# Hybrid trunk on one core: first squares folded on VectorE, first modulation group by k tile, rstd read from PSUM

## The chip, the cores and the metric

The kernel runs on one core of one Trainium2 chip. The metric is the device time of one execution in microseconds (us); lower is better. A core has five engines with a queue each, which run in parallel and wait for each other by semaphores: TensorE (PE, matmuls from SBUF into PSUM), VectorE (DVE), ScalarE (ACT), GpSimd (POOL) and SyncE (SP, which here issues the DMA transfers). Each queue is worked off in its own order.

## What is computed

Two layers of a decoder trunk over 256 tokens of width 2048, in float32:

```python
c_act = silu(c)
for l in range(2):
    shift, scale, gate = split(c_act @ w_ada[l] + b_ada[l], 3)
    h = rms_norm(x, norm_w[l]) * (1 + scale) + shift
    gq, gk, gv, ..., aq, ak, av, az = split(h @ w_in[l])
    o = concat(gated_linear_attention, gated_delta_net, differential_attention)   # each normed and gated
    x = x + gate * (o @ w_out[l])
```

`w_ada` is 2048 x 6144 per layer (the modulation), `w_in` 2048 x 7704 (the input projection), `w_out` 2048 x 2048.

## The kernel before

Tokens lie on the free axis of `xt` (128 features x 16 k tiles x 256 tokens). All weights are streamed from HBM in pieces of 128 x 1024 (512 KB) through six buffers of one pool (`raw` for projections, `rawa` for modulation, both with the tag "raw").

**Projections** are made in split precision: `weights` loads a piece, ScalarE casts it to `wh` (fp32r), VectorE makes the rest `wl = raw - wh`; three buffers each. `project` then issues per k tile three matmuls, `wh`x`hh`, `wl`x`hh` and `wh`x`hl`, where `hh` and `hl` are the two halves of the modulated h, made by `modulate`: VectorE multiplies x, the rstd row and the scale (`hn`), ScalarE adds the shift (`hh`), VectorE takes the rest (`hl`). `BLOCKS` lists 28 blocks of output columns (18 to 27 are token blocks `aq`, `ak`, `av`, `gz`, `dz`, `az` of 512 columns) and `STEPS` the groups of blocks and k tiles in which they are done: in layer 0 first blocks 18 to 27 on k tiles 0 and 1 ("group 0"), then the same on k tiles 2 and 3 ("group 1"), then the rest. `in_chunks` cuts a group into pieces of 1024: in group 0 one block with both k tiles per piece, ten pieces, 12 matmuls each. The accumulators `pt` and `pf` share four PSUM banks (tag "p"); the first group of a block is copied out by ScalarE, later ones are added by VectorE (`evac_`).

**Modulation** runs on VectorE: each piece of `w_ada` is multiplied by the row of c (`c_row`) and summed along its columns (`ada_group`, the line with `accum_out`); eight pieces make a group, and four small ScalarE instructions finish it (`ada_j`). Groups 0 to 7 of a layer give scale and shift of two k tiles each, groups 8 to 11 the gates. The pieces of a layer's first group 0 (`fr`) are loaded at the very start; all others are spread over the program by `advance` and `pace`.

**rstd** (`rstd_rows`): the squares of x are made by ScalarE in four quarters and folded by GpSimd, TensorE sums them over partitions into `ss`, ScalarE and GpSimd (`row_power`) make r, ScalarE spreads r on the diagonal of `dg`, TensorE multiplies ones by it into `rstd_ps`, and ScalarE copies that to `rb` in SBUF, which `modulate` reads. In layer 1 the squares come from the end of layer 0's output projection.

The GLA, GDN and attention parts run as generators between the projections' pieces (`poll`). The tile framework's scheduler sets each engine's order from the code's order, priorities (`AHEAD`, `URG`) and its own simulated times; only matmuls that share an accumulator group are pinned by hand (`in_order`). Small constants (`load_constants`: the rest of `ct`, `adb`, `posi`) are loaded when the first block is done.

Of the kernel before, what the change touches and what calls it, by code (L numbers as in the profile page):

```python
# [75 lines left out]
def in_chunks(layer, i):  # L76

    b0, b1, k0, k1 = STEPS[layer][i]
    out = []
    for b in range(b0, b1):  # L80
# [60 lines left out]
def hybrid_trunk(ctx: ExitStack, tc: tile.TileContext, x, cvec, pos, par, w_ada, w_in, w_out, w_lr, qkn, adt, cst, out):  # L141
# [91 lines left out]
    in_order = lambda: tc.manual_schedule(engines={mybir.EngineType.PE})  # L233
# [3 lines left out]
    SP.dma_start(pt, par)  # L237
# [8 lines left out]
    SP.dma_start(ct[:, 0:128], cst[:, 0:128])  # L246
# [3 lines left out]
    first_raws = []  # L250
# [39 lines left out]
    state = {"n": 0}  # L290

    def weights(src, n):

        raw = wraw.tile([P, RAW], F32, name="raw", tag="raw")[:, 0:n]
        wh = wsp.tile([P, RAW], F32R, name="wh", tag="wh")[:, 0:n]
        wl = wsp.tile([P, RAW], F32R, name="wl", tag="wl")[:, 0:n]
        with tc.high_priority(offset=AHEAD if state["n"] else 0):
            SP.dma_start(raw, src)
# [3 lines left out]
        state["n"] += 1  # L302
        return wh, wl

# [8 lines left out]
    def ada_group(l, g, raws=None):  # L313

        sums = tiny("ada_p", 8)
        for i in range(8):
            if raws is None:
                raw = wraw.tile([P, RAW], F32, name="rawa", tag="raw")[:, 0:1024]
                with tc.high_priority(offset=AHEAD):
                    SP.dma_start(raw, w_ada[l, g, i])  # L320
            else:
                raw = raws[i]
            cb = c_row[:, 1024 * (i % 2):1024 * (i % 2) + 1024]
            with tc.high_priority(offset=AHEAD):
                DVE.scalar_tensor_tensor(raw, raw, 1.0, cb, ALU.mult, ALU.mult, accum_out=sums[:, i:i + 1])  # L325
            if i < 7:
                yield
        for f in range(4):
            if g < 8:
                k = 2 * g + f % 2  # L330
                j = 0 if f < 2 else 1
            else:
                k = 4 * (g - 8) + f
                j = 2
            o, scale = ada[l][:, j, k:k + 1], pcol("norm", 16 * l + k) if j == 0 else 1.0
            bias = pcol("b_ada", 48 * l + (16, 0, 32)[j] + k)
            ACT.activation(tiny("ada_j", 2), sums[:, 2 * f:2 * f + 2], AF.Identity, bias=bias, scale=scale, accum_out=o)  # L337
        yield

    def ada_all():  # L340
        for l in range(L):
            for g in range(12):
                yield from ada_group(l, g, first_raws if l == 0 and g == 0 else None)

    ada_it = ada_all()
    ada_n = [0]
# [14 lines left out]
    def rstd_rows(sqs):  # L361
# [21 lines left out]
    def modulate(l, xt, rb, hh, hl, k):  # L383

        for i in range(k, k + 2):
            h = reg(i % 4, "hn")[:, 0:T]
            scale, shift = ada[l][:, 0, i:i + 1], ada[l][:, 1, i:i + 1]
            DVE.scalar_tensor_tensor(h, rb, scale, xt[:, i, :], ALU.mult, ALU.mult)
            ACT.activation(hh[:, i, :], h, AF.Identity, bias=shift)  # L389
            DVE.scalar_tensor_tensor(hl[:, i, :], h, shift, hh[:, i, :].bitcast(F32), ALU.add, ALU.subtract)  # L390


    in_off = [0]
# [894 lines left out]
```

## Time and profile before

| | |
|---|---|
| median of 3 runs (lowest, highest) | 1103.11 us (1100.97, 1106.03) |
| the profiled execution's own time | 1103.98 us |
| its span in the profile | 1102.2 us |
| busy PE, DVE, ACT, POOL | 1047.0, 888.6, 607.2, 219.8 us |
| moved by DMA | 273.24 MB, mean 248 GB/s |

A busy share is an average over stages with different limits; a matmul's end is modelled, so TensorE counts as busy while matmuls overlap. "Idle before" in brackets says how long the engine stood still before an instruction and what ended that. In a group of matmuls the spacing of their starts, not their length, is the rate.

### The profile page before, as it was taken

What the parts mean: (1) busy time and instruction counts of PE and PEld (TensorE: products, weight loads), DVE (VectorE), ACT (ScalarE), POOL (GpSimd) and SP (SyncE); (2) the same over time, 40 slices, a digit from 0 to 9 for tenths busy, and PEclk for the clock granted to TensorE, in tenths of its full rate; (3) what the DMA queues carried; (4) which work ended last, traced back from release to release, by engine and by line L of the source; (5) the groups of instructions that cost most, each with busy time, mean ns of one, the idle gap of its engine ahead of it and who ended that gap; (6) DMA issues with size and microseconds to landing.
All of it is one profiled execution on the core that took longest, in us unless ns stands there. A gap on an engine that the chain in (4) does not pass through costs nothing.

```text
span 1102.2 us, 19699 instructions
## 1 busy us (share of the span) xinstructions
PE 1047.0 (95%) x7398; PEld 918.9 (83%) x7398; DVE 888.6 (81%) x1365; ACT 607.2 (55%) x1251; POOL 219.8 (20%) x284
## 2 busy tenths in 40 slices
PE   4999999999899989999979999999999999999998
PEld 3768888889898777898977877899989877889998
DVE  5899999998999886888687776677756776787874
ACT  4745544447765646466545555468444556557742
POOL 4000000040130841134210000024222144102400
PEclk9999999999999999999998999999999999999999
DMA  9888999999877545755588888796535645777472
GB/s 352 311 299 308 351 336 341 329 296 339 301 270 254 182 145 188 249 162 186 167 318 327 308 315 319 238 306 228 181 116 174 218 164 172 246 244 236 136 216 90
DMA packets 76799, 273.24 MB, mean 248 GB/s; under 512 B 8816, under 2 KB 9888, under 8 KB 76576
## 3 DMA queue, kind: packets, MB, share of 16 engines
q1 hardware_dynamic: 76704, 271.99, 71.7%
q8 instruction: 58, 0.95, 0.3%
q14 instruction: 37, 0.30, 0.1%
HBM read 267.76 MB, written 4.19 MB: 247 GB/s over the span
## 4 chain that ended last, share of the span: by engine, by line
PE 55%; DVE 18%; DMA 11%; issue 9%; ACT 5%; POOL 2%; SPq 0%; DVEq 0%; ACTq 0%; POOLq 0%
PE pt L180 20%; PE py L180 12%; PE pf L180 12%; DMA rawa<-in_w_ada 8%; DVE wl L301 6%; DVE rawa L325 5%; DMA raw<-in_w_in 2%; ACT wh L300 2%; PE Z_ps L180 1%; PE o_gdn L180 1%; DVE fr L325 1%; PE s_ps L180 1%; DVE aqk L436 1%; DVE z L436 1%; PE o_diff L180 1%
## 5 line engine op out<-in xcount | busy, mean ns | idle before, releaser
L300 ACT CAST wh<-raw 128x1024 fp32r<-128x1024 f32 (+1 forms) x312 | 320.0, 1028 | 272.9 <-PE pt L180 119.4
L301 DVE TENSOR_TENSOR wl<-raw,wh 128x1024 fp32r<-128x1024 f32 (+1 forms) x312 | 384.1, 1236 | 72.2 <-ACT wh L300 68.9
L180 PE MATMUL pt<-wl,hh 128*128 128x512 f32 (+1 forms) x768 | 293.5, 383 | 5.4 <-DVE wl L301 5.4
L180 PE MATMUL pt<-wh,hl 128*128 128x512 f32 (+1 forms) x768 | 291.7, 382 | 0.0
L325 DVE SCALAR_TENSOR_TENSOR rawa<-rawa,c_row 128x1024 f32<-128x1024 f32 x184 | 229.1, 1250 | 74.6 <-DMA rawa<-in_w_ada 74.3
L180 PE MATMUL pt<-wh,hh 128*128 128x512 f32 (+1 forms) x768 | 273.1, 383 | 8.5 <-ACT hh L389 4.3
L180 PEld LDWEIGHTS pt<-wh,hh 128*128 128x128 f32 x768 | 145.3, 191 | 40.6 <-ACT hh L389 5.7
L180 PEld LDWEIGHTS pt<-wl,hh 128*128 128x128 f32 x768 | 145.9, 190 | 38.3 <-DVE wl L301 10.4
L180 PEld LDWEIGHTS pt<-wh,hl 128*128 128x128 f32 x768 | 146.0, 190 | 28.7 <-issue 0.2
L180 PE MATMUL pf<-hh,wl 128*128 128x256 f32 x512 | 143.4, 283 | 3.5 <-DVE wl L301 3.5
L180 PE MATMUL pf<-hh,wh 128*128 128x256 f32 x512 | 144.3, 282 | 1.7 <-ACT wh L300 1.6
L180 PE MATMUL pf<-hl,wh 128*128 128x256 f32 x512 | 144.1, 282 | 0.0
L180 PE MATMUL py<-ogg,wh 128*128 128x256 f32 x512 | 101.1, 291 | 1.2 <-DVE xr L1183 0.6
L180 PEld LDWEIGHTS pf<-hh,wl 128*128 128x128 f32 x512 | 95.6, 188 | 6.0 <-DVE wl L301 4.2
L180 PEld LDWEIGHTS pf<-hh,wh 128*128 128x128 f32 x512 | 96.1, 188 | 3.1 <-ACT wh L300 1.8
L180 PEld LDWEIGHTS pf<-hl,wh 128*128 128x128 f32 x512 | 96.0, 188 | 1.5 <-issue 1.0
L180 PE MATMUL py<-odf,wh 128*128 128x256 f32 x512 | 91.4, 282 | 1.4 <-ACT odf L1028 1.0
L180 PEld LDWEIGHTS py<-ogg,wh 128*128 128x128 f32 x512 | 81.4, 190 | 3.2 <-DVE xr L1183 0.8
L180 PEld LDWEIGHTS py<-odf,wh 128*128 128x128 f32 x512 | 79.0, 190 | 2.5 <-ACT odf L1028 1.5
L337 ACT ACTIVATE ada_j<-ada_p,pt 128x2 f32<-128x2 f32 x96 | 31.1, 324 | 80.5 <-DVE rawa L325 72.8
L180 PE MATMUL py<-odf,wl 128*128 128x256 f32 x256 | 71.9, 282 | 1.4 <-DVE wl L301 1.3
L180 PE MATMUL py<-ogg,wl 128*128 128x256 f32 x256 | 72.7, 285 | 0.0
(277 smaller groups left out, 1335.9 us busy)
## 6 DMA issues: line engine op xcount, KB each, us to landing
raw<-in_w_in SPq DMA_DIRECT2D x224, 512.0 KB, 4.8
rawa<-in_w_ada SPq DMA_DIRECT2D x184, 512.0 KB, 4.8
raw<-in_w_out SPq DMA_DIRECT2D x64, 512.0 KB, 4.2
raw<-in_w_in SPq DMA_DIRECT2D x20, 402.0 KB, 4.4
fr<-in_w_ada SPq DMA_DIRECT2D x8, 512.0 KB, 10.6
xt<-in_x SPq DMA_DIRECT2D x4, 512.0 KB, 5.6
xr<-in_x SPq DMA_DIRECT2D x4, 512.0 KB, 8.2
xs<-xr SPq DMA_DIRECT2D x1, 2048.0 KB, 10.2
```

The costliest lines, as they stand in the source:

```text
L180: return PE.matmul(o, lhsT=lhsT, rhs=rhs, start=start, stop=stop, **kw)
L300: ACT.copy(wh, raw)
L301: DVE.tensor_tensor(wl, raw, wh.bitcast(F32), ALU.subtract)
L325: DVE.scalar_tensor_tensor(raw, raw, 1.0, cb, ALU.mult, ALU.mult, accum_out=sums[:, i:i + 1])
L337: ACT.activation(tiny("ada_j", 2), sums[:, 2 * f:2 * f + 2], AF.Identity, bias=bias, scale=scale, accum_out=o)
L436: DVE.tensor_tensor(d, src, d, ALU.add)
```

## The change

- `squares`: the fold of the four quarters moves from GpSimd to VectorE, with a last add that leaves one tile of 256 columns instead of two; all at high priority. All four `c_row` copies are VectorE's.
- Loads: `pt` and the first part of `ct` are issued from ScalarE's queue; x is issued right behind c. The eight `fr` pieces come in the order 0, 1, 4, 5, first weight piece, 2, 3, 6, 7, second weight piece.
- The first modulation group is finished k tile by k tile, in an order that is written by hand for VectorE and ScalarE: pieces 0, 1, 4, 5 give scale and shift of k tile 0.
- `in_chunks`: the first two pieces of group 0 hold blocks 18 and 19 on k tile 0, then on k tile 1, so that two blocks (four PSUM banks) are open at once; pieces three to ten are as before.
- rstd: two matmuls with r, broadcast, against the identity write `rstd_ps`; `dg` and the copy `rb` are gone, and `modulate` reads PSUM, in both layers.
- `load_constants` is issued behind the last weight load of group 0.

```diff
@@ in_chunks
+    if (layer, i) == (0, 0):
+
+        out = [[(b0, k, k + 1), (b0 + 1, k, k + 1)] for k in range(k0, k1)]
+        b0 += 2
@@ start of hybrid_trunk
-    SP.dma_start(pt, par)
     SP.dma_start(c16, cvec)
-    SP.dma_start(ct[:, 0:128], cst[:, 0:128])
+    ACT.dma_start(ct[:, 0:128], cst[:, 0:128])
+    ACT.dma_start(pt, par)
...
     for q in range(2):
         fr = t16("fr", [P, 4, 1024])
         for i in range(4):
-            SP.dma_start(fr[:, i, :], w_ada[0, 0, 4 * q + i])
-            first_raws.append(fr[:, i, :])
+            n = 4 * (i // 2) + 2 * q + i % 2
+            SP.dma_start(fr[:, i, :], w_ada[0, 0, n])
+            first_raws[n] = fr[:, i, :]
+        load_first()
...
-        (ACT.copy if i % 2 else DVE.tensor_copy)(c_row[:, 512 * i:512 * i + 512], cb)
+        DVE.tensor_copy(c_row[:, 512 * i:512 * i + 512], cb)
@@ rstd_rows
-        dg = reg(8, "dg")[:, 0:T]
-        pb = bank("rstd_ps", "a")
-        rb = small.tile([P, T], F32, name="rb", tag="rb", bufs=1)
+        rb = bank("rstd_ps", "a")[:, 0:T]
...
             for t in range(2):
-                ACT.activation(dg[:, 128 * t:128 * t + 128], ident, AF.Copy, scale=r[:, t:t + 1])
-            mm(pb[:, 0:T], ones, dg)
-            ACT.copy(rb, pb[:, 0:T])
+                mm(rb[:, 128 * t:128 * t + 128], r[:, t:t + 1].broadcast_to([P, P]), ident)
@@ squares of x
-            POOL.tensor_tensor(p[:, 0:2, :], p[:, 0:2, :], p[:, 2:4, :], ALU.add)
+            DVE.tensor_tensor(p[:, 0:2, :], p[:, 0:2, :], p[:, 2:4, :], ALU.add)
             if q > 0:
-            POOL.tensor_tensor(sqx[:, 0:2, :], sqx[:, 0:2, :], p[:, 0:2, :], ALU.add)
-    sq = [sqx[:, 0, :], sqx[:, 1, :]]
+                DVE.tensor_tensor(sqx[:, 0:2, :], sqx[:, 0:2, :], p[:, 0:2, :], ALU.add)
+        last_fold = DVE.tensor_tensor(sqx[:, 0, :], sqx[:, 0, :], sqx[:, 1, :], ALU.add)
+    sq = [sqx[:, 0, :]]
@@ before the projections of layer 0
+            def cast(i, a, z):
+                ACT.copy(first[i][0][:, a:z], loaded[i][:, a:z])
+            def split(i):
+                DVE.tensor_tensor(first[i][1], loaded[i], first[i][0].bitcast(F32), ALU.subtract)
+                done_first.append(first[i])
+            def meanwhile(i):
+                cast(i, 512 * (1 - i), RAW)
+                if i == 0:
+                    product(2)
+                split(i)
+            with tc.high_priority(offset=AHEAD), in_order(mybir.EngineType.DVE, mybir.EngineType.Activation):
+                with tc.issue_after(last_fold.ins):
+                    product(0)
+                product(1)
+                product(4)
+                cast(0, 0, 512)
+                product(5)
+                modulate(0, xt, rb, hh, hl, 0, lambda: meanwhile(0))
+                for n in (3, 6, 7):
+                    product(n)
+                modulate(0, xt, rb, hh, hl, 1, lambda: meanwhile(1))
...
+            if l == 0 and i == 1:
+                with tc.issue_after(last_dma[0].ins):
+                    load_constants()
```

`product(n)` is one modulation product of the first group, with its small ScalarE instruction behind every second one; `modulate` now takes one k tile and calls `meanwhile` between its `hh` and its `hl`.

VectorE at the start of layer 0, before (`fr` is a piece of the first modulation group, `wl` the rest of a weight piece):

```order
L287 COPY c_row_83<-c_ps_120 128x512
L287 COPY c_row_83<-c_ps_132 128x512
L325 SCALAR_TENSOR_TENSOR fr_93,ada_p_167<-fr_93,c_row_83 128x1024 x4
L325 SCALAR_TENSOR_TENSOR fr_98,ada_p_167<-fr_98,c_row_83 128x1024 x4
L388 SCALAR_TENSOR_TENSOR hn_210<-rb_196,ada0_144,xt_88 128x256
L388 SCALAR_TENSOR_TENSOR hn_214<-rb_196,ada0_144,xt_88 128x256
L301 TENSOR_TENSOR wl_220<-raw_218,wh_219 128x1024
L390 SCALAR_TENSOR_TENSOR hl_204<-hn_210,ada0_144,hh_203 128x256
L390 SCALAR_TENSOR_TENSOR hl_204<-hn_214,ada0_144,hh_203 128x256
L325 SCALAR_TENSOR_TENSOR rawa_266,ada_p_265<-rawa_266,c_row_83 128x1024
```

and now:

```order
L1087 TENSOR_TENSOR sqx_158<-sqx_158 128x512 x2
L1088 TENSOR_TENSOR sqx_158<-sqx_158 128x256
L331 SCALAR_TENSOR_TENSOR fr_93,ada_p_192<-fr_93,c_row_82 128x1024 x4
L403 SCALAR_TENSOR_TENSOR hn_208<-rstd_ps_180,ada0_148,xt_88 128x256
L331 SCALAR_TENSOR_TENSOR fr_100,ada_p_192<-fr_100,c_row_82 128x1024
L1191 TENSOR_TENSOR wl_194<-raw_98,wh_193 128x1024
L406 SCALAR_TENSOR_TENSOR hl_186<-hn_208,ada0_148,hh_185 128x256
L331 SCALAR_TENSOR_TENSOR fr_100,ada_p_192<-fr_100,c_row_82 128x1024 x3
L403 SCALAR_TENSOR_TENSOR hn_222<-rstd_ps_180,ada0_148,xt_88 128x256
L331 SCALAR_TENSOR_TENSOR rawa_262,ada_p_261<-rawa_262,c_row_82 128x1024
L1191 TENSOR_TENSOR wl_196<-raw_105,wh_195 128x1024
L406 SCALAR_TENSOR_TENSOR hl_186<-hn_222,ada0_148,hh_185 128x256
```

The fold stands ahead of the first products, `hn` of k tile 0 has moved ahead of four of the eight, and one weight piece is split between the two k tiles.

TensorE at the same place, before (`ss` and `rstd_ps` are rstd's sums and its spread, `pt` the accumulators of group 0):

```order
L180 MATMUL ss<-ones,sqx 128x1 x4
L180 MATMUL rstd_ps<-dg,ones 128x256
L180 MATMUL pt<-wh,hh 128x512 x2
L180 MATMUL pt<-wl,hh 128x512 x2
L180 MATMUL pt<-wh,hl 128x512 x2
```

and now:

```order
L184 MATMUL ss<-ones,sqx 128x1 x2
L184 MATMUL rstd_ps<-ct,rs 128x128 x2
L184 MATMUL pt<-wh,hh 128x512 x4
L184 MATMUL pt<-wl,hh 128x512 x4
L184 MATMUL pt<-wh,hl 128x512 x4
```

The first piece is twelve matmuls of k tile 0 for two blocks, ordered by operand; rstd's sum has half the matmuls.

GpSimd in the GDN and attention part of layer 0, where no code is edited (`C` is a masked copy of GDN's matrix, `r_d` and `scr` belong to the attention's norm and rotation, `on_gdn` to GDN's queries), before:

```order
L812 TENSOR_TENSOR on_gdn<-fm 128x512 x2
L783 TENSOR_TENSOR C<-Lm,ct 128x512
L923 TENSOR_TENSOR scr<-aqk,rtab 128x4x64 x2
L906 TENSOR_SCALAR r_d<-r_d 128x8
L359 TENSOR_TENSOR r_d<-r_d,mhalf 128x8
```

and now:

```order
L941 TENSOR_TENSOR scr<-aqk,rtab 128x4x64 x2
L830 TENSOR_TENSOR on_gdn<-fm 128x512
L924 TENSOR_SCALAR r_d<-r_d 128x8
L379 TENSOR_TENSOR r_d<-r_d,mhalf 128x8
L801 TENSOR_TENSOR C<-Lm,ct 128x512
```

`C` has moved behind the rotation and behind `r_d` with its power.

## Rows read from the trace of the kernel before

**Rows 1.** Busy time by stage: start:end, length, then busy us and count per engine.
```profile
27.00:57.00 30.00, 29.89 (x121) 23.85 (x122) 24.19 (x35) 22.54 (x42) 0.00 (x0) 1.00 0.86 314
57.00:97.00 40.00, 36.14 (x171) 28.06 (x170) 39.40 (x60) 17.76 (x31) 0.00 (x0) 1.00 0.82 280
```

**Rows 2.** Timeline of the start, x: start, length, engine, line, what, idle before.
```profile
2.09 1.86 SPq L249 DMA_DIRECT2D xt<-in_x  x4
...
11.60 1.06 ACT L1065 ACTIVATE sqx<-xt 128x1024 f32<-128x1024 f32 x1 [1.42 <-DMA xt<-in_x]
```

**Rows 3.** Timeline of the start, from the row of c to group 0.
```profile
3.63 7.16 PE L180 MATMUL c_ps<-c,ct 16*128 16x128 f32 x32
...
12.99 2.08 DVE L325 SCALAR_TENSOR_TENSOR fr<-fr,c_row 128x1024 f32<-128x1024 f32 x1 [3.18 <-DMA fr<-in_w_ada]
13.96 4.45 POOL L1068 TENSOR_TENSOR sqx<-sqx 128x512 f32<-128x512 f32 x2
...
18.46 1.87 PE L180 MATMUL ss<-ones,sqx 128*128 128x1 f32 x8 [7.67 <-POOL sqx L1068]
...
21.38 0.97 POOL L359 TENSOR_TENSOR rs<-ms,mhalf 128x2 f32<-128x2 f32 x1 [2.98 <-ACT ms L375]
...
24.00 1.21 DVE L325 SCALAR_TENSOR_TENSOR fr<-fr,c_row 128x1024 f32<-128x1024 f32 x1
...
25.15 0.87 DVE L388 SCALAR_TENSOR_TENSOR hn<-rb,ada,xt 128x256 f32<-128x256 f32 x2
...
25.61 1.03 ACT L300 CAST wh<-raw 128x1024 fp32r<-128x1024 f32 x1
26.55 0.90 ACT L389 ACTIVATE hh<-hn,ada 128x256 fp32r<-128x256 f32 x2
...
27.11 1.22 PE L180 MATMUL pt<-wh,hh 128*128 128x512 f32 x2 [2.75 <-ACT hh L389]
```

**Rows 4.** Busy time in group 0, its first matmuls apart.
```profile
27.00:30.60 3.60, 3.50 (x8) 2.66 (x9) 3.60 (x6) 2.33 (x4) 0.00 (x0) 1.00 0.94 320
30.60:57.00 26.40, 26.40 (x114) 21.19 (x113) 20.59 (x30) 20.21 (x38) 0.00 (x0) 1.00 0.85 313
```

**Rows 5.** Groups of instructions by line and shape, whole span: busy us, mean ns.
```profile
L1183 DVE SCALAR_TENSOR_TENSOR xr<-py,ada,xr 128x256 f32<-128x256 f32 x96 | 45.2, 477 | 23.6 <-PE py L180 19.9 <-DMA xr<-xs 3.4
...
L436 DVE TENSOR_TENSOR aqk<-pt,aqk 128x512 f32<-128x512 f32 x40 | 25.9, 679 | 0.1
...
L388 DVE SCALAR_TENSOR_TENSOR hn<-rb,ada,xt 128x256 f32<-128x256 f32 x16 | 7.5, 475 | 0.0
```

**Rows 6.** Timeline of the layer boundary, from the power to the first `hn`.
```profile
578.48 0.69 ACT L378 ACTIVATE dg<-ct,rs 128x128 f32<-128x128 f32 x2 [0.82 <-POOL rs L359]
...
579.20 1.22 DVE L325 SCALAR_TENSOR_TENSOR rawa<-rawa,c_row 128x1024 f32<-128x1024 f32 x1
...
579.22 1.22 PE L180 MATMUL rstd_ps<-dg,ones 128*128 128x256 f32 x2 [1.87 <-ACT dg L378]
...
580.48 0.37 ACT L380 COPY rb<-rstd_ps 128x256 f32<-128x256 f32 x1 [0.75 <-PE rstd_ps L180]
580.89 1.67 DVE L388 SCALAR_TENSOR_TENSOR hn<-rb,ada,xr 128x256 f32<-128x256 f32 x4 [0.45 <-ACT rb L380]
```

**Rows 7.** TensorE by stretch: length, busy us and count, granted clock, DMA share, GB/s.
```profile
236.60:238.40 1.80, 0.07 (x2) 1.00 0.67 179
238.40:239.00 0.60, 0.60 (x5) 0.98 1.01 322
239.00:242.40 3.40, 3.40 (x17) 0.50 0.93 267
```

**Rows 8.** Timeline of SP's queue: issues of the constants and of weights.
```profile
20.57 0.33 SPq L489 DMA_DIRECT2D ct<-in_cst  x1
...
45.18 0.33 SPq L298 DMA_DIRECT2D raw<-in_w_in  x1
```

**Rows 9.** Timeline of TensorE in layer 0's attention part, RoPE transposes.
```profile
395.53 1.58 PE L184 MATMUL ropeT_ps<-ct,scr 128*128 128x128 f32 x8 [3.42 <-DVE scr L925]
```

More of the change, by code (lines that the diff above doesn't have):

```diff
@@ L249, in hybrid_trunk, with load_first @@
         SP.dma_start(xt0[:, 4 * q:4 * q + 4, :], x[:, 4 * q:4 * q + 4, :])
-    first_raws = []
+    first_raws, loaded, in_off = {}, [], [0]
+    def load_first():
+        raw = wraw.tile([P, RAW], F32, name="raw", tag="raw")
+        SP.dma_start(raw, w_in[in_off[0]:in_off[0] + P * RAW].rearrange("(p n) -> p n", p=P))
+        in_off[0] += P * RAW
+        loaded.append(raw)
     for q in range(2):
@@ L311, in hybrid_trunk, with ada_product, ada_finish, ada_group @@
                                  ALU.add, ALU.mult)
-    def ada_group(l, g, raws=None):
+    def ada_product(raw, i, sums):
+        cb = c_row[:, 1024 * (i % 2):1024 * (i % 2) + 1024]
+        with tc.high_priority(offset=AHEAD):
+            DVE.scalar_tensor_tensor(raw, raw, 1.0, cb, ALU.mult, ALU.mult, accum_out=sums[:, i:i + 1])
+    def ada_finish(l, g, sums, f):
+        if g < 8:
+            k = 2 * g + f % 2
+            j = 0 if f < 2 else 1
+        else:
+            k = 4 * (g - 8) + f
+            j = 2
+        o, scale = ada[l][:, j, k:k + 1], pcol("norm", 16 * l + k) if j == 0 else 1.0
+        bias = pcol("b_ada", 48 * l + (16, 0, 32)[j] + k)
+        ACT.activation(tiny("ada_j", 2), sums[:, 2 * f:2 * f + 2], AF.Identity, bias=bias, scale=scale, accum_out=o)
+    def ada_group(l, g):
         sums = tiny("ada_p", 8)
         for i in range(8):
[L317 to L323, printed above, removed]
+            raw = wraw.tile([P, RAW], F32, name="rawa", tag="raw")[:, 0:1024]
             with tc.high_priority(offset=AHEAD):
-                DVE.scalar_tensor_tensor(raw, raw, 1.0, cb, ALU.mult, ALU.mult, accum_out=sums[:, i:i + 1])
+                SP.dma_start(raw, w_ada[l, g, i])
+            ada_product(raw, i, sums)
             if i < 7:
@@ L342, in ada_all @@
             for g in range(12):
-                yield from ada_group(l, g, first_raws if l == 0 and g == 0 else None)
+                if (l, g) != (0, 0):
+                    yield from ada_group(l, g)
     ada_it = ada_all()
-    ada_n = [0]
+    ada_n = [8]
     def ada_to(n):
@@ L377, in rstd_rows, with modulate @@
             for t in range(2):
-                ACT.activation(dg[:, 128 * t:128 * t + 128], ident, AF.Copy, scale=r[:, t:t + 1])
-            mm(pb[:, 0:T], ones, dg)
-            ACT.copy(rb, pb[:, 0:T])
-        return rb
[L383 to L393, printed above, removed]
+                mm(rb[:, 128 * t:128 * t + 128], r[:, t:t + 1].broadcast_to([P, P]), ident)
+        return rb
+    def modulate(l, xt, rb, hh, hl, k, between=lambda: None):
+        h = reg(k % 4, "hn")[:, 0:T]
+        scale, shift = ada[l][:, 0, k:k + 1], ada[l][:, 1, k:k + 1]
+        DVE.scalar_tensor_tensor(h, rb, scale, xt[:, k, :], ALU.mult, ALU.mult)
+        ACT.activation(hh[:, k, :], h, AF.Identity, bias=shift)
+        between()
+        DVE.scalar_tensor_tensor(hl[:, k, :], h, shift, hh[:, k, :].bitcast(F32), ALU.add, ALU.subtract)
     class Out:
@@ L1091, in advance @@
                     with tc.high_priority(offset=AHEAD):
-                        modulate(l, xt, rb, hh, hl, mod[0])
+                        for k in range(2):
+                            modulate(l, xt, rb, hh, hl, mod[0] + k)
                     mod[0] += 2
@@ L1100, in block_done @@
             lo, hi = span
-            if l == 0 and b == STEPS[0][0][0] and len(seen) == 0:
-                seen.add("constants")
-                load_constants()
             advance(lo + int((hi - lo) * done))
@@ L1158, in after, with product @@
             yield from gen
+        if l == 0:
+            sums = tiny("ada_p", 8)
+            def product(n):
+                ada_product(first_raws[n], n, sums)
+                if n % 2 == 1:
+                    ada_finish(0, 0, sums, n // 2)
+            first = [[wsp.tile([P, RAW], F32R, name=n, tag=n) for n in ("wh", "wl")] for _ in range(2)]
+            def cast(i, a, z):
[19 more added lines that the diff above has]
+                modulate(0, xt, rb, hh, hl, 1, lambda: meanwhile(1))
+            mod[0] = 2
         for i, (b0, b1, k0, k1) in enumerate(STEPS[l]):
+            if l == 0 and i == 1:
+                with tc.issue_after(last_dma[0].ins):
+                    load_constants()
             advance(ada_mark(l, (k1 - 1) // 2))
```

39 lines of the change are left out of this document (17 added, 22 removed).

## The prediction, made before the changed kernel ran

> **What bounds the kernel now.** I read the stretches by stage first, then the start instruction by instruction, then the layer boundary, then the places where TensorE stands still later on. TensorE carries this kernel, so a change at the start is worth what it moves TensorE's work forward, provided that the stage behind it moves too.
>
> In layer 0, group 0 (ten token blocks on k tiles 0 and 1, 120 matmuls of 512 columns) begins at 27.11 [rows 3]. Its first 8 matmuls take 3.6 us, 0.45 us each; after that 114 begin in 26.4 us, 0.232 us each, with TensorE busy throughout while VectorE has 20.59 and ScalarE 20.21 us of work in it [rows 4]. So group 0 is bound by TensorE, and it ends at about 27.1 + 3.5 + 112 x 0.232 = 56.6. The next stretch, 57 to 97, is bound by VectorE (39.40 of 40.00 us busy, TensorE 36.14) [rows 1]. VectorE there does the splits and evictions of a group that TensorE's progress lets begin, and in group 0 it has 5.8 us to spare, so what TensorE gains in group 0 VectorE gains as well.
>
> Why not before 27.11? The last quarter of x reaches ScalarE's square at 11.60 [rows 2]. GpSimd then folds the squares until 18.41, TensorE's sum follows at 18.46, the power at 21.38 [rows 3]. Beside it VectorE multiplies the eight tiles of the first modulation group, the first at 12.99 and taking 2.08 us while GpSimd folds, the last at 24.00 in 1.21 us; it is free for the first `hn` at 25.15. That end, not rstd, is last. A cast of weights (1.03 us) and `hh` stand between it and the first matmul [rows 3].
>
> **The change part by part.** *Fold on VectorE.* x moves up two places in SP's queue, from 2.09 by two steps of 0.46 us (1.86 for four) [rows 2], so its last quarter lands at an estimated 10.7 (at 11.6 if the transfer and not the issue sets it; the range keeps both). Square 1.06 us: 11.75. Behind the last square VectorE has three adds of 512 columns and one of 256. A 512-column add costs 0.65 (25.9 us for 40), a 256-column pass 0.40 (two `hn`, 0.87, less the overlap) [rows 5, 3]: 2.35 us, done at 14.1. The fourth `c_row` copy, now VectorE's too, waits for `c_ps`, which ends at 10.79 [rows 3], so it is out of the way. What goes is GpSimd's 4.45 us at the end of its fold and the stretched products beside it (2.08 against 1.21).
>
> *First group by k tile.* The products now stand behind the last fold on VectorE. Tiles 0, 1, 4, 5, which finish scale and shift of k tile 0, are loaded first: 14.1 + 4 x 1.15 (24.00 to 25.15) = 18.7. rstd is ready sooner: half of the 1.87 us sum, the power's 0.97 and 1.22 us of TensorE [rows 3, 6] end near 17.5. `hn` 0.40, `hh` 0.50 (two take 0.90 with their overlap): the first matmul at 19.65, 7.5 us earlier. But it covers k tile 0 alone. The half cast behind `hh`, product 2, split and `hl` follow on VectorE until 21.8, in time for the twelve matmuls, which at 0.45 us last until 25.05. For k tile 1 VectorE still owes products 3, 6, 7 (25.25) and `hn` (25.65); ScalarE then owes `hh` (26.15) and the whole cast, 1.03, which its queue holds behind `hh`: 27.2. So the second k tile starts where all the work started before, with 12 of 120 matmuls done.
>
> *What twelve matmuls are worth* hangs on TensorE's clock. It idles some 2 us in between. [...] I expect the same: 0.6 us with 2 matmuls, 3.4 us with 8, then 98 x 0.232 = 22.7, in all 26.7. The two blocks open at once hold all four of their PSUM banks, so the next block waits for a copy, half of a 1.03 us cast at most; I take 0.4. End at 54.3 against 56.6: 2.3 us gained. If the clock stays up, 108 x 0.232 = 25.1, 0.8 us of waiting for splits and the 0.4 give 53.5: 3.1 us. I take 2.3, since the row with the nearest gap shows the fall.
>
> *Constants later.* Their three loads leave the start, where 0.5 MB at 20.57 was followed by the two small ones, and go behind the tenth weight load, which was issued at 45.18 [rows 8]. `ea`, `posf` and `nexpa` wait for them on ScalarE and VectorE, behind them casts and evictions. DMA has 0.15 of 26.4 us free there [rows 4], 4.0 us, against 0.5 MB / (313/0.85 GB/s) = 1.4 us. I take nothing, and 1.4 us for the range.
>
> *rstd from PSUM.* At the layer boundary two scaled copies (0.69) and the copy `rb` (0.37) leave the path. `hn` at 580.89 could begin 1.1 us earlier, but VectorE is held by a product from 579.20 for 1.22 us, until 580.42 [rows 6], and the order there keeps it in front. So 0.5 us. The 32 reads from PSUM instead of SBUF I take at nothing: the same instruction on 256 columns takes 477 ns with a PSUM source (`xr<-py`) and 475 from SBUF [rows 5].
>
> [...]
>
> *The order further on.* Nothing is edited there, but the GDN and attention part of layer 0 comes out in another order on GpSimd, VectorE and TensorE. Its nearest price is the stall at 395.53, where TensorE's queue stood 3.42 us at the RoPE transposes [rows 9], and a fall of the clock as in [rows 7], half of 3.4 us: 5.1 us, to gain or to lose. No row says which; I take 0.
>
> **Sum.** 2.3 + 0.5 = 2.8 us. The profiled execution took 1103.98 us (span 1102.2), the median of the runs is 1103.11, so 1101.2 as a profile and **1100.3** as a median.
>
> **The rivals.** *One: the stall in the middle goes* as a by-product of the new order, as the transposes now mix with other small matmuls. 1100.3 - 5.1 = 1095.2 if all of it goes, 1097.7 for half. For it: the wait was on VectorE's queue, which is rearranged there. Against: the work on it is the same.
>
> *Two, the slower side: that stall grows.* GpSimd now does `r_d` and its power ahead of the mask product `C`, and GDN's next step waits for `C`. If TensorE's queue stands there twice as long with a second fall of the clock, 1100.3 + 5.1 = 1105.4. It decides from 2.8 us more of standing still. Against: TensorE is ahead by then.
>
> *Three: the gain is swallowed before 100 us.* Either x lands at 11.6 or later after all, which moves everything from the fold on (0.9 us), or the constants delay the weights that group 1 needs (1.4 us): 1100.3 + 2.3 = 1102.6, no change to speak of. Likewise if the first k tile's matmuls do not come ahead, and the change does not do what it says.
>
> *Four: reads from PSUM are dear.* VectorE is the bound from 57 to 97, so a longer `hn` would count: at a tenth of its 0.48 us, 32 x 0.048 = 1.5 us, 1101.8. The rows of equal length speak against it.
>
> [...]
>
> **How the numbers follow.** Forecast 0.47 (1098.5 to 1102 by the two clock cases and the spread of the runs), rival one 0.20, two 0.12, three 0.16, four 0.05. The range runs from rival one's end to rival two's, 1095 to 1105.5, and leaves out less than 2 in 10. A measurement of this kernel can tell about 0.5%, 5.5 us. Below 1097.6 lie most of rival one and a little of the forecast: 0.22. Above 1108.6 lies only a stall dearer than any seen: 0.04. Within: 0.74.
>
> **What would show it.** First matmul near 19.7, twelve of them, a gap of about 2 us, the next near 27.2, a stretch at 0.50 granted clock behind it, and group 0's 120 matmuls over at about 54. Products near 1.2 us each, none above 2. At the boundary `hn` straight behind the last product. If the second k tile comes before 25 or after 29, the count on VectorE was wrong; if group 0 ends at 54 and the whole ends nowhere near 3 us sooner, the stage behind did not follow, or the new order in the middle decided.

## The result, and the profile after

The changed kernel is slower. Its median is 1115.6 us (4 runs, 1112.2 to 1118.8) against 1104.6 us for the kernel before on the same chip (4 runs); the ratio is 1.0104, with a 95% interval from 1.0064 to 1.0145. The profiled execution took 1112.23 us with a span of 1110.3, 8.1 us more than the 1102.2 before. It is the fastest of its four, so the profiles show 8.1 of the 11.0 us between the medians. I had forecast 1100.3.

The start first, as the timeline has it (start, length, engine, line, what, idle time before and what ended it):

```profile
1.17 0.45 ACTq L250 DMA_DIRECT2D pt<-in_par  x1
...
5.84 0.16 DVE L288 TENSOR_TENSOR lp<-pt 128x4 f32<-128x4 f32 x1 [4.86 <-DMA pt<-in_par]
...
6.58 7.19 PE L184 MATMUL c_ps<-c,ct 16*128 16x128 f32 x32
...
16.99 1.22 DVE L331 SCALAR_TENSOR_TENSOR fr<-fr,c_row 128x1024 f32<-128x1024 f32 x1
...
22.71 2.08 PE L184 MATMUL pt<-wh,hh 128*128 128x512 f32 x4 [1.52 <-ACT hh L404]
24.58 1.97 PE L184 MATMUL pt<-wl,hh 128*128 128x512 f32 x4
26.35 1.41 PE L184 MATMUL pt<-wh,hl 128*128 128x512 f32 x4
30.24 1.91 PE L184 MATMUL pt<-wh,hh 128*128 128x512 f32 x4 [2.49 <-ACT wh L1188]
```

The shape is the one predicted: twelve matmuls, a gap, the second k tile, every product at 1.22 us. But all of it is about 3 us late. The parameters `pt`, now the second load on ScalarE's queue, are first read at 5.84. TensorE takes the small `lam_ps` matmuls that need them ahead of `c_ps`, so the row of c begins at 6.58 instead of 3.63 [rows 3], and VectorE's copies of it spread between the folds. The issues by transfer say the same (KB each, us from issue to landing), first of the kernel before, then of after:

```profile
pt<-in_par SPq DMA_DIRECT2D x1, 122.0 KB, 2.0
```
```profile
pt<-in_par ACTq DMA_DIRECT2D x1, 122.0 KB, 4.7
```

The stages that answer to [rows 1] (start:end, length, busy us and count of TensorE, weight loads, VectorE, ScalarE, GpSimd, granted clock, DMA share, GB/s):

```profile
27.00:57.00 30.00, 27.51 (x110) 21.51 (x110) 24.14 (x37) 22.81 (x43) 0.00 (x0) 0.94 0.87 315
57.00:97.00 40.00, 36.38 (x171) 28.07 (x170) 40.00 (x61) 17.53 (x31) 0.00 (x0) 1.00 0.81 269
```

So nothing is won at the start, but little is lost: 300 us later the two kernels are within 1 us of each other (the first `G_ps` matmul of GDN at 315.6 before, 316.6 after). The loss lies behind that, in the middle of layer 0, where no line was edited. TensorE's share of it can be added up from six stretches (start:end, length, TensorE's busy time and matmuls, granted clock, DMA share, GB/s). First before, then after:

```profile
300.00:380.00 80.00, 80.00 (x845) 1.00 0.71 241
380.00:440.00 60.00, 55.05 (x419) 0.97 0.52 169
440.00:480.00 40.00, 39.28 (x310) 1.00 0.67 226
480.00:520.00 40.00, 38.61 (x291) 0.96 0.58 181
520.00:560.00 40.00, 38.13 (x304) 0.96 0.54 183
560.00:600.00 40.00, 31.45 (x159) 0.83 0.92 342
```
```profile
300.00:380.00 80.00, 78.70 (x732) 1.00 0.76 248
380.00:440.00 60.00, 55.58 (x489) 0.91 0.51 163
440.00:480.00 40.00, 38.37 (x296) 1.00 0.68 228
480.00:520.00 40.00, 35.10 (x267) 0.91 0.36 109
520.00:560.00 40.00, 37.02 (x295) 1.00 0.58 189
560.00:600.00 40.00, 32.31 (x205) 0.83 0.90 336
```

TensorE stands for 17.5 us of the 300 before (300 less the sum of the busy times) and for 22.9 after: 5.4 us. The part of its busy time that the granted clock took away, an estimate (busy time by one less the clock, summed), is 10.1 us before and 13.7 after: 3.6 us. Together 9.0 us, and rstd's matmul at the boundary between the layers begins 8.9 us later (579.22 in [rows 6], 588.12 now). Layer 1 gives 0.8 us of it back.

Where does the standing come from? TensorE's waits between 300 and 560 (whom it waited for, us, times, longest):

```profile
PE Y_ps L184 <- DVE Um L811: 3.7, 1, 3.7
PE aT_ps L188 <- DVE scr L983: 3.4, 1, 3.4
```

The stall at the RoPE transposes of [rows 9] is gone (400.56, no idle time before it), and others stand in its place. Behind the first of them is a queue. What GpSimd and VectorE do there, and the matmul that waits for it:

```profile
395.34 1.29 POOL L801 TENSOR_TENSOR C<-Lm,ct 128x512 f32<-128x512 f32 x1
...
396.60 1.03 POOL L662 TENSOR_TENSOR mix<-scr,ss_gla 128x512 f32<-128x512 f32 x1
...
397.66 0.76 DVE L941 TENSOR_TENSOR scr<-aqk,rtab 128x256 f32<-128x256 f32 x2 [5.59 <-POOL mix L662]
398.34 1.22 DVE L331 SCALAR_TENSOR_TENSOR rawa<-rawa,c_row 128x1024 f32<-128x1024 f32 x1
399.49 0.42 DVE L811 TENSOR_TENSOR Um<-Um,Z_ps 128x256 f32<-128x256 f32 x1
```
```profile
400.05 0.48 PE L184 MATMUL Y_ps<-Um,C 64*64 64x64 f32 x4 [3.73 <-DVE Um L811]
```

GDN's `Um` needs `Z_ps`, whose last matmuls began at 389.89 and took 1.10 us. It begins at 399.49, because a RoPE step ahead of it in VectorE's queue waits 5.59 us for GpSimd's `mix` and a product of 1.22 us follows. `Y_ps` also reads `C`, which GpSimd ends at 396.63; so 0.3 us of TensorE's 3.73 are `C`'s and 3.4 are the queue's. In the kernel before the longest such wait of a RoPE step for GpSimd is 2.2 us. This step of `Um`, the third of four, comes 15.8 us later than before (399.49 against 383.65), the one ahead of it already 8.9 us (378.72 against 369.81).

The second wait, at 490.64, is the attention's own latency (scores, maximum, exponential, combination): between 486 and 490.6 TensorE has a single transpose and no output projection beside it, and in 480 to 520 it is busy 35.1 us instead of 38.6. GDN's chain ends later, the attention behind it begins later, and the last output projection of layer 0 (`py<-odf`) with it. One tile's rows, before and then after (min/median/max ns; first and last start):

```profile
L180 PE MATMUL s_ps<-aqk x96: 270/275/422, 467.7 to 1021.6; 128*128 128x128 f32 x96
...
L180 PE MATMUL py<-odf,wh x512: 276/276/467, 515.7 to 1098.3; 128*128 128x256 f32 x171
```
```profile
L184 PE MATMUL s_ps<-aqk x96: 270/275/377, 483.4 to 1029.7; 128*128 128x128 f32 x96
...
L184 PE MATMUL py<-odf,wh x512: 276/276/467, 526.9 to 1106.5; 128*128 128x256 f32 x171
```

The scores begin 15.7 us later, the last output projection 11.2 us.

The two programs show why a step can come later without being longer. Of VectorE's 618 instructions of layer 0 behind its first step, the same 618 in both, 36 are GDN's. Counting how many of the other 582 stand ahead of each: `Um` behind `CT_ps` has 330 before and 332 after, the first update of `Um` 351 and 355, `E` behind `QK_ps` 367 and 375, the fourth update of `Um` 384 and 400, the first `vn` 421 and 435, the last 440 and 455. Most of these places are splits, products and evictions of 0.4 to 1.2 us.

### The profile page after: what moved, and what is told of

Read it like the earlier page. It is cut to its first block, busy times and chain, and to the rows that moved or that the text cites. A ratio compares the mean times of both kernels' runs of the same rounds, so it can differ in the third digit from the quotient of the medians.

```text
span 1110.3 us, 19684 instructions
## 1 busy us (share of the span) xinstructions
PE 1051.1 (95%) x7398; PEld 918.9 (83%) x7398; DVE 892.6 (80%) x1375; ACT 604.1 (54%) x1244; POOL 209.2 (19%) x277
## 4 chain that ended last, share of the span: by engine, by line
PE 51%; DVE 22%; DMA 10%; issue 10%; ACT 5%; POOL 2%; DVEq 0%; ACTq 0%; POOLq 0%
PE pt L184 21%; PE py L184 12%; DMA rawa<-in_w_ada 9%; PE pf L184 8%; DVE wl L315 8%; DVE rawa L331 7%; ACT wh L314 2%; DMA raw<-in_w_in 1%; PE o_gdn L184 1%; DVE z L451 1%; DVE aqk L451 1%; PE Z_ps L184 1%; DVE on_gdn L675 1%; PE ropeT_ps L188 1%; PE s_ps L184 1%
## 5 line engine op out<-in xcount | busy, mean ns | idle before, releaser
L314 ACT CAST wh<-raw 128x1024 fp32r<-128x1024 f32 (+2 forms) x310 | 318.2, 1029 | 293.4 <-PE pt L184 131.9
L315 DVE TENSOR_TENSOR wl<-raw,wh 128x1024 fp32r<-128x1024 f32 (+2 forms) x310 | 383.0, 1241 | 68.1 <-ACT wh L314 67.3
L184 PE MATMUL pt<-wh,hh 128*128 128x512 f32 (+1 forms) x768 | 272.9, 385 | 10.1 <-ACT hh L404 3.2
## 6 DMA issues: line engine op xcount, KB each, us to landing
xs<-xr SPq DMA_DIRECT2D x1, 2048.0 KB, 10.1
```

Of the source, the lines that this page charges most:

```text
L184: return PE.matmul(o, lhsT=lhsT, rhs=rhs, start=start, stop=stop, **kw)
L314: ACT.copy(wh, raw)
L315: DVE.tensor_tensor(wl, raw, wh.bitcast(F32), ALU.subtract)
```

## The experiments

The theory after these readings: the edits cost nothing to speak of, and the loss is the new issue order in the middle of layer 0, which comes out differently because the scheduler plans everything behind the edit anew. The rival: the edits themselves cost it (late parameters, rows of rstd held in a PSUM bank, weights two places elsewhere), and the order is a symptom.

To separate them, an order can be written down and imposed. Behind the first step of layer 0 both kernels trace the same instructions in the same sequence on every engine (618 on VectorE, 457 on ScalarE, 140 on GpSimd, 256 transfers of SP, 3110 matmuls), so the issue order of one is a permutation that fits the other (the code is shortened; what stands in brackets after `mine =` and inside the call stands for code):

```diff
 for l in range(L):
+    if l == 1:
+        impose_order(tc, since[0], ORDER0)
     rb = rstd_rows(sq)
...
+        if (l, i) == (0, 1):
+            since[0] = tc.nc.cur_bb.bb.instructions[-1]
         project(l, i, hh, hl, o, block_done)
...
+def impose_order(tc, first, order):
+    mine = (what was traced since first)
+    for e, text in order.items():
+        seq = [i for i in mine if i.engine == names[e]]
+        perm = [int(n) for n in text.split()]
+        for a, b in zip(perm, perm[1:]):
+            tc.add_manual_dep(seq[b], seq[a].name, (NoSync: order of issue alone, no wait), reason="order")
```

All kernels below, sorted by their profiled span, which is the last column. The three columns before it are starts in that execution: the first one for the scores and the last output projection, the last one for rstd of layer 1; all in us.

| kernel | median us | ratio to before, 95% | scores | last output projection | rstd, layer 1 | span |
|---|---|---|---|---|---|---|
| before_pt_l1 | 1100.21 | 0.9963 (0.9946 to 0.9980) | 467.7 | 514.0 | 577.1 | 1095.8 |
| pt_old_order | 1100.19 | 0.9959 (0.9937 to 0.9981) | 467.4 | 515.4 | 578.9 | 1098.0 |
| rstd_pt_l1 | 1102.58 | 0.9980 (0.9959 to 1.0001) | 472.5 | 518.8 | 582.2 | 1101.3 |
| after_old_order | 1104.63 | 0.9996 (0.9977 to 1.0014) | 470.0 | 516.4 | 579.6 | 1101.4 |
| before | 1104 to 1105 | 1 | 467.7 | 515.7 | 579.8 | 1102.2 |
| after_pt_l1 | 1099.96 | 0.9971 (0.9948 to 0.9994) | 469.3 | 517.3 | 581.4 | 1102.3 |
| after_dve_old | 1105.54 | 1.0019 (0.9997 to 1.0041) | 473.7 | 521.6 | 584.1 | 1103.9 |
| rstd_old_order | 1110.49 | 1.0068 (1.0040 to 1.0096) | 472.5 | 520.4 | 583.4 | 1108.7 |
| rstd_psum_alone | 1110.22 | 1.0034 (1.0008 to 1.0060) | 469.8 | 517.8 | 581.2 | 1108.9 |
| after_pe_old | 1110.92 | 1.0062 (1.0039 to 1.0085) | 478.0 | 524.3 | 588.0 | 1109.1 |
| after | 1115.6 | 1.0104 (1.0064 to 1.0145) | 483.4 | 526.9 | 588.9 | 1110.3 |
| after_chain_old | 1117.03 | 1.0132 (1.0097 to 1.0166) | 481.7 | 529.3 | 592.7 | 1114.0 |
| after_gdn_old | 1121.12 | 1.0152 (1.0126 to 1.0177) | 475.4 | 533.4 | 597.8 | 1120.2 |
| before_new_order | 1119.73 | 1.0116 (1.0093 to 1.0138) | 488.0 | 532.2 | 597.8 | 1120.8 |
| before_chain_new | 1125.62 | 1.0203 (1.0173 to 1.0233) | 487.3 | 531.8 | 596.4 | 1123.2 |
| start_alone | 1127.75 | 1.0196 (1.0176 to 1.0215) | 486.7 | 530.6 | 598.6 | 1126.0 |

**The order, both ways.** `after_old_order` is the changed kernel in the old order of layer 0, `before_new_order` the kernel before in the new one.

> The changed kernel, start and rstd as changed, but from the second step of layer 0 to the end of layer 0 the instructions of each engine are chained in the order in which the kernel before issues them (618 on VectorE, 457 on ScalarE, 140 on GpSimd, 256 DMAs of SP, 3110 on TensorE; order alone, no waits). Theory A, the loss is the new issue order in the middle of layer 0: the markers of layer 0 are back at the places of the kernel before (Y1 near 346 us instead of 353, ropeT near 395.5 instead of 400.6, u near 421 instead of 437), and the time is 1102 to 1106 us. Theory B, the edits themselves cost it (the late parameters, the rows of rstd held in a PSUM bank, the two places by which weights and DMAs stand otherwise): the order does not matter and the time stays at 1112 to 1119 us, with Y1 still near 353.

> The kernel before, start and rstd as they were, with the same stretch of layer 0 chained in the order of the changed kernel. Theory A (the order costs the time): 1112 to 1119 us, with Y1 near 353 us and u near 437. Theory B (the edits themselves cost it): 1101 to 1106 us, as the kernel before, Y1 near 346.

Both come out as the order says: 0.9996 and 1.0116 (1119.73 us, just above the range that I had given), though the edits would have it the other way round. In the changed kernel with the old order, 1.0104 has become no difference. `Y_ps` did not come back to 346 us, as I had written, but to 348.7: the late start is carried along, by 2.7 us at `Y_ps` and 2.3 at the scores, until it meets the end of the attention (0.7 us at the last output projection). That the order is the cause of the loss is shown in both directions; the rival falls.

**One edit at a time.** `rstd_psum_alone` is the kernel before with the rstd edit; `start_alone` is the changed kernel with the old path of rstd.

```diff
-    rb = small.tile([P, T], F32, name="rb", tag="rb", bufs=1)
+    rb = bank("rstd_ps", "a")[:, 0:T]
...
-            ACT.activation(dg[:, 128 * t:128 * t + 128], ident, AF.Copy, scale=r[:, t:t + 1])
-        mm(pb[:, 0:T], ones, dg)
-        ACT.copy(rb, pb[:, 0:T])
+            mm(rb[:, 128 * t:128 * t + 128], r[:, t:t + 1].broadcast_to([P, P]), ident)
```

> The kernel before with one edit: the rows of rstd are made by two matmuls with rstd as a broadcast weight and read from PSUM; the start is as before. Theory A: the order of layer 0 is nearly that of the kernel before, so 1102 to 1106 us, less the 0.5 us that I gave this edit. Theory B in the form that the PSUM reads or the held bank cost it: 1112 us or more.

> The changed kernel with the old path of rstd (two scaled copies of the identity, one matmul, a copy to SBUF): the start alone is changed. Theory A: the order of layer 0 on VectorE is nearly that of the changed kernel, so 1112 to 1119 us. Theory B in the form that the PSUM rows cost it: 1102 to 1106 us.

Neither landed where I said: 1110.2 us lies between the two theories, and 1127.7 us is above both. Half of the change is worse than the whole of it. With the order left to the scheduler, an edit can also be a new draw of the order, so taking an edit out alone does not measure the edit. In `rstd_psum_alone` layer 0 comes out in the order of the kernel before (VectorE, GpSimd and TensorE have no two instructions swapped between the traces, counted from 70 to 575 us) and is over at 581.2, 1.4 us behind it. The other 5.3 of its 6.7 us are lost in layer 1, which is ordered anew. In `start_alone` VectorE's order of layer 0 is nearly the changed kernel's, as I had supposed (83 swapped pairs, where the changed kernel and the one before differ in about 760). Yet its layer 0 ends 9.7 us later than the changed kernel's (598.6 against 588.9, single executions), and its layer 1 takes 6.0 us longer. Why the first of these is so stays open: at the old order the edits cost nothing to speak of, at the new one they were not priced.

**One engine's order.** The changed kernel with the old order of VectorE alone, and of TensorE alone (`ORDER0` holds one engine).

> The changed kernel with VectorE's 618 instructions of layer 0 (from its second step) chained in the order of the kernel before; the other engines are left to the scheduler. If the loss sits in VectorE's queue (GDN's short steps standing behind more conv, split and product work): 1102 to 1108 us. If it sits in TensorE's queue (GDN's matmuls standing behind more projection): 1110 to 1119 us.

> The changed kernel with TensorE's 3110 matmuls of layer 0 (from its second step) chained in the order of the kernel before; the other engines are left to the scheduler. If the loss sits in VectorE's queue: 1110 to 1119 us. If it sits in TensorE's queue: 1102 to 1108 us. If either order alone draws the others after it, since the scheduler plans them around it, both kernels come near 1105.

VectorE's order alone brings the loss from 1.04% to 0.19%, TensorE's to 0.62%. But neither kernel isolates an engine, since the scheduler plans the others around the one that is held, which the expectation had as its third case. Counted in the traces from 70 to 575 us, GpSimd comes back to 3 swapped pairs out of 51 in both, and VectorE, left free beside TensorE's old order, to 128 out of about 760. So with TensorE's order as of old and these pairs left 0.62% stay lost, with VectorE's as of old 0.19%. That points at VectorE's queue and does not show it; the orders of GpSimd and ScalarE were not tried alone.

**The start with its parameters early.** The changed kernel in the old order of layer 0, with one line moved:

```diff
+    SP.dma_start(pt, par)          # ahead of c16
...
-    ACT.dma_start(pt, par)
```

> The changed kernel in the old order of layer 0, with the parameters (pt) issued first on SP's queue again instead of behind ct on ScalarE's. If the late parameters are what cost the start its gain: the table row of c is spread by 4 us, the fold ends near 14 us, the first matmul of group 0 stands near 19.7 us instead of 22.7, and the time is 2 to 3 us below the same kernel with the late parameters, 1101.5 to 1103 us. If the weight stream bounds the first 200 us (DMA share 0.92 to 0.96 there), the first matmul moves as well but by 200 us the lead is gone, and the time is that of the kernel before, 1104 to 1106 us. If the order of DMAs matters (pt ahead of x delays x): the first matmul stays near 22 us.

1100.19 us, below all that I had written down, and the start is nearly the one that I had predicted. The rows are ScalarE's last square, VectorE's last copy of the row of c and its first product, TensorE's first matmuls on each k tile, and a wait near the end of group 0. The two single rows are TensorE's stretch behind the gap, first here, then in the changed kernel (busy time and matmuls, granted clock, DMA share, GB/s):

```profile
10.04 1.06 ACT L1084 ACTIVATE sqx<-xt 128x1024 f32<-128x1024 f32 x1 [0.22 <-DMA xt<-in_x]
...
11.98 0.68 DVE L301 COPY c_row<-c_ps 128x512 f32<-128x512 f32 x1
...
14.37 1.22 DVE L331 SCALAR_TENSOR_TENSOR fr<-fr,c_row 128x1024 f32<-128x1024 f32 x1
...
20.08 2.07 PE L184 MATMUL pt<-wh,hh 128*128 128x512 f32 x4 [1.51 <-ACT hh L404]
...
27.62 2.07 PE L184 MATMUL pt<-wh,hh 128*128 128x512 f32 x4 [2.91 <-ACT wh L1191]
...
52.37 0.59 ACT L449 COPY z<-pt 128x512 f32<-128x512 f32 x1 [1.51 <-PE pt L184]
...
54.21 1.23 DVE L315 TENSOR_TENSOR wl<-raw,wh 128x1024 fp32r<-128x1024 f32 x1 [2.65 <-ACT wh L314]
```
```profile
27.62:33.62 6.00, 6.00 (x14) 0.50 0.87 253
```
```profile
30.60:34.00 3.40, 3.40 (x10) 0.52 0.84 234
```

The slow stretch lasts 6.0 us here. So group 0 ends 1.2 us earlier than in the kernel before, not 2.3. Its last matmul, the 120th on `pt`, before and here (the changed kernel has it at 57.09):

```profile
56.62 0.39 PE L180 MATMUL pt<-wh,hl 128*128 128x512 f32 x1
```
```profile
55.44 0.39 PE L184 MATMUL pt<-wh,hl 128*128 128x512 f32 x1
```

And this lead does not last. The rows of TensorE's first wait in the VectorE-bound stage (57 to 97 us, VectorE busy 39.40 us before [rows 1] and 39.45 here), before and here:

```profile
69.69 0.50 PE L180 MATMUL pt<-wl,hh 128*128 128x512 f32 x1 [0.64 <-DVE wl L301]
```
```profile
68.62 0.50 PE L184 MATMUL pt<-wl,hh 128*128 128x512 f32 x1 [0.63 <-DVE wl L315]
```

1.07 us are left there, and about 0.4 from 111 us on: between 97 and 115 us the DMA share is 0.99 in both kernels, and from 95 to 135 ScalarE's casts wait 2.0 us for weights here against 0.3 before. The first `gcb_ps` of GDN begins at 302.5 against 302.6, the scores at 467.4 against 467.7. So the 4 us by which this kernel beats the one before must come from elsewhere; that 1100.19 is close to the 1100.3 of my forecast is luck. From the last rstd matmul of layer 1 to its last `gcb_ps` (768.7 here, 773.4 before) it takes 3.8 us less, in a layer whose order was free.

**The order of layer 1.** `before_pt_l1` is the kernel before with none of the edits, layer 0 in its own order and layer 1 in the order of that kernel. `after_pt_l1` is the changed kernel, late parameters and all, with both orders.

> The kernel before without any of the edits, layer 0 in its own order and layer 1 chained in the order that the changed kernel with early parameters came out with (that one took 1100.19 us; its layer 1 ran 3 us shorter between 579 and 769 us than that of the kernel before). If that kernel's gain of 4 us is the order of layer 1: 1099.5 to 1102 us here too. If it is the start and rstd: 1103 to 1106 us, as the kernel before.

> The changed kernel, late parameters and all, with both layers chained in the order of the kernel that took 1100.19 us; only the queue and the place of the parameters' load differ from that one. If the early parameters are worth what TensorE gains at the start: 2 to 3 us above it, 1102 to 1103.5 us. If whatever is won at the start is lost again by the boundary of the layers: 1099.5 to 1101 us.

1100.21 and 1099.96 us, beside the 1100.19 of `pt_old_order`. Without any edit the imposed orders give the same 0.37%, so the gain is not the edits'. What in them gives it stays open. Compared in the traces, layer 1 of `pt_old_order` and of the kernel before differ in 7 swapped pairs on VectorE, 7 on ScalarE, 94 on TensorE and none on GpSimd or among SP's loads. In `after_gdn_old` (below) layer 1 came out with 2 pairs on VectorE, 2 on ScalarE and none on TensorE swapped against `pt_old_order`, and takes 522.4 us instead of 519.1 in the profiles. The kernel before with layer 1 held in its own order was not run, so a few places, the holding itself and scatter are not told apart. The three kernels, at equal order, are the price list of the edits: their intervals reach from 0.9937 to 0.9994, so start, early or late, and rstd together move the time by less than about 0.4% either way. The profiles put the late parameters at 2.5 us (rstd of layer 1 at 581.4 against 578.9) in this pair, but at 0.7 us in `after_old_order` (579.6), whose layer 0 has the same order; the medians don't show them.

**rstd at a fixed order.**

> The kernel before with the rstd edit alone and with layer 0 chained in the order of the kernel before. Before it, the rstd edit alone took 1110.2 us with its order left to the scheduler. If the reads of PSUM or the held bank cost time themselves: 1108 to 1112 us again. If it was the order: 1103.5 to 1105.5 us (0.2 us gained at the boundary between the layers, 0.4 us at the start), with whatever the free order of layer 1 adds.

> The kernel before with the rstd edit alone, both layers chained in the order of the kernel that took 1100.19 us. With the order of layer 1 left to the scheduler it took 1110.5 us. If the PSUM rows of rstd cost nothing themselves: within 1 us of the kernel before in this same order (0.2 us below it, by the boundary). If the reads of PSUM or the bank that they hold cost time: 3 us or more above it.

With layer 1 free 1110.5 us, with layer 1 pinned 1102.6 us, 2.4 us above `before_pt_l1` with overlapping intervals, between the two cases that I had written. A cost of the PSUM rows of more than some 5 us is excluded, one of 1 or 2 us is not. In these two profiles TensorE's clock falls (0.91 from 436 to 476 us) in a place where it doesn't in the same order without the edit (1.00 in `before_pt_l1`, last section), and 3 us are lost there. The edit alone does not bring the fall: `after_old_order` has it too, with the same order of layer 0, and no fall there.

**Which of VectorE's instructions.** Three kernels move a part of VectorE's order, counted by how many of the others stand ahead: GDN's 36 steps put back in the changed kernel; GDN's, the attention's and the gates' 128 put back; and those 128 put at their new places in the kernel before.

> The changed kernel with VectorE's order of layer 0 as it is, but for 36 of its 618 instructions: GDN's own steps (Lm, C, Tm, Um, vn, S and the like), which in the changed kernel stand up to 16 places further back among the conv, split, eviction and product work than in the kernel before, are put back behind as many other instructions as in the kernel before. The other 582 keep the changed kernel's order; the other engines are left to the scheduler. If GDN's chain waiting in VectorE's queue is the mechanism: most of the loss goes, 1104 to 1109 us, and u stands near 421 to 428 us instead of 437. If it is the rest of the order (which weights and products are done when): 1111 to 1119 us.

> The changed kernel with VectorE's order of layer 0 as it is, but for 128 of its 618 instructions: the steps of GDN, of the attention's norms, RoPE and softmax and of the gates, the dependent chain, are put back behind as many other instructions as in the kernel before. The other 490 (splits, products, evictions, conv, output sums) keep the changed kernel's order; the other engines are left to the scheduler. If the place of the chain among the bulk work carries the loss: 1103 to 1108 us, attention's scores begin near 470 us and the last output projection of layer 0 near 517. If the order of the bulk work carries it: 1110 us or more, as with GDN's 36 steps alone.

> The mirror image: the kernel before, VectorE's order of layer 0 as it is, but the same 128 steps of the dependent chain stand behind as many other instructions as in the changed kernel. If the place of the chain carries the loss: 1110 to 1117 us, GDN ends near 480 us instead of 467 and the last output projection begins near 527 instead of 516. If the order of the bulk work carries it: 1103 to 1107 us.

The first two should have gained if the place of the chain's steps were the whole story, and both lost; 1121.12 us is above both cases that I had written. The 128 steps make most of the difference between the two orders: with them put back, VectorE's differs from the old one in 155 pairs instead of 780, and still 1.3% is lost. So it is not the amount of reordering that counts. `after_gdn_old` in the stretches shown above, and its longest wait of TensorE:

```profile
440.00:480.00 40.00, 37.29 (x267) 0.91 0.58 198
480.00:520.00 40.00, 30.18 (x215) 0.83 0.37 110
```
```profile
PE oT_ps L188 <- DVE scr L967: 5.2, 1, 5.2
```

GDN did end sooner, and the scores began at 475.4 instead of 483.4. But the attention then took 58.0 us to its last projection (475.4 to 533.4) instead of 43.5: the gap of TensorE at 480 to 520 grew from 4.9 to 9.8 us, with the clock at 0.83. My reading, which no run shows by itself: a step put back to an old place among other work that stands in a new sequence meets neither its inputs nor its readers there. The mirror image lost as well (1.0203), more than the 1117 us that I had allowed for. So which of VectorE's instructions carry the loss stays open: not the chain's places alone, and the bulk work's sequence alone was not tried.

## Why the prediction was wrong, point by point

- **The step that failed: the order further on, taken at 0.** I had its price, 5.1 us either way from the worst stall of [rows 9] and one fall of the clock, and thought of it as one place. It is a chain of places. The scores begin 15.7 us later, and the sum of standing (5.4 us) and clock (3.6 us) is 9.0 us at the boundary. Among the kernels here, which do nearly the same work, that boundary moves from 577 to 599 us, of which some 3 us are scatter (577.1 and 579.8 have one order of layer 0). A bound from the sum over the stalls of the stage, and not from its largest, would have been nearer. Rival two named the right kind of event with a wrong place and price: the wait for `C` is there, but it is 0.3 us, hidden behind VectorE's queue, which the rival did not have.
- **The fold, mis-sized by one wait.** Forecast: first product at 14.1, first matmul at 19.65, second k tile at 27.2. Measured: 16.99, 22.71, 30.24, each about 3 us late, and with the parameters early 14.37, 20.08, 27.62. The step left out is that `pt`, moved from SP's queue to the second place on ScalarE's, is read by `lam_ps` in front of `c_ps`. "Out of the way" was said of a `c_ps` that ended at 10.79; it ends at 13.8. With the parameters early the working comes out within 0.5 us, in part by luck: the last square ends at 11.10, before my 11.75, and the fourth copy of `c_row` is not out of the way but stands in the fold at 11.98 and takes 0.6 us.
- **Twelve matmuls and the clock: the fall right, its length not.** With the early parameters TensorE idles 2.9 us and then runs at 0.50 from the first matmul on: 6.0 us with 14 matmuls, where I had 0.6 us and then 3.4 us with 8, after the stretches at 0.98 and 0.50 in [rows 7]. So group 0's last matmul begins at 55.44, not 54.3, and the term of 2.3 us measures 1.2. In the changed kernel the slow stretch is 3.4 us at 0.52, as I had it, behind an idle time of 2.5 us; in the kernel before TensorE idled 2.75 us [rows 3] and ran on at 1.00 [rows 4]. How long a fall lasts I could not have read from the one row that I used.
- **"What TensorE gains in group 0 VectorE gains as well": held, for the 1.2 us that there were.** With the early parameters VectorE's splits lead by 3.0 us at 49.5. At 52.37 ScalarE's copy of a finished block waits 1.51 us for TensorE, the next cast stands behind it, and VectorE waits 2.65 us for that. From then to 95 us its lead is 1.06 to 1.08 us, that of TensorE. What the sentence left out is the stretch behind, from 97 to 115 us, where the DMA share is 0.99 in both kernels: 0.4 us are left from 111 us on, 0.3 at the scores. Rival three had the outcome, for other reasons.
- **Constants later: right** at nothing to speak of: `ea` is 0.21 us on ScalarE at 50.05 (`pt_old_order`), and none of the waits above is theirs.
- **rstd at the boundary: half of it.** At equal order (`after_old_order` against [rows 6]) the eight last matmuls of the sum begin together, 575.50 and 575.49, and the first `hn` at 580.67 against 580.89: 0.2 us gained, not 0.5, because a product began 0.3 us later and holds VectorE until then.
- **32 reads from PSUM at nothing: right.** The groups by shape (busy us, mean ns), with the PSUM source, in `after_old_order`:

```profile
L403 DVE SCALAR_TENSOR_TENSOR hn<-rstd_ps,ada,xt 128x256 f32<-128x256 f32 x16 | 7.7, 480 | 0.7 <-ACT ada_j L342 0.7
L403 DVE SCALAR_TENSOR_TENSOR hn<-rstd_ps,ada,xr 128x256 f32<-128x256 f32 x16 | 7.2, 478 | 0.0
```

480 and 478 ns against 475 from SBUF [rows 5]: 5 and 3 ns more for each read, where rival four had 48; it falls.
- **The chances.** 0.04 for slower was the error that mattered. The slower rival had one place as its price, so "a stall dearer than any seen" looked unlikely; the sum of several ordinary ones was not.

## What to carry to other kernels

Where a scheduler plans the order, an edit can also be a new draw of the order behind it, and a draw can be worth more than the edit: here nearly the same work spans 1100 to 1128 us. Before an edit is judged, impose the old order on what was not edited and compare at equal order; the price holds for that order. A good draw can be kept in the same way, as the kernel at 1100.2 us without any edit suggests. When such a change is forecast, the reordered stage needs its own range, from the sum of its chain's waits and not from its longest, and an early load that moves to another queue has to be followed to its first reader.

## What was not expected of the hardware

- A 122 KB load issued at 1.17 us as the second on ScalarE's queue, beside four 512 KB loads of SP's, took 4.7 us (`after`); issued at 0.72 as the first on SP's it took 2.0 (`before`) and 2.5 us (`pt_old_order`). Whether the queue or the time of issue does it was not separated.
- TensorE's clock fell to 0.53 in one kernel and stayed at 1.00 in the other at the same place of the same order. In `rstd_pt_l1` and `before_pt_l1` layer 0 is issued in one order on all engines. TensorE's stretches there, first of the one, then of the other, then of `after_old_order`, which has the rstd edit and that order too:

```profile
442.60:446.00 3.40, 3.40 (x19) 0.53 1.03 394
446.00:450.00 4.00, 4.00 (x21) 0.55 1.02 405
```
```profile
436.00:450.00 14.00, 13.45 (x100) 1.00 0.87 338
```
```profile
440.00:450.00 10.00, 9.45 (x72) 1.00 1.00 370
```

Before the fall the first two had the same waits (0.3 us for `vn`). From there the scores are 4.8 us late instead of 1.7. Part of the scatter of single executions (1097.6 to 1105.4 us for `before_pt_l1`) may be such falls; that was not shown.
